# Three banks of PSUM for transposes and two for projections in a two-layer decoder trunk

## The chip, the cores and the metric

The kernel runs on one core of a Trainium2 chip. The metric is the device time of one execution in microseconds. Five engines take part: TensorE (PE in the profile; its weight loads are PEld), VectorE (DVE), ScalarE (ACT), GpSimd (POOL) and SyncE (SP), which issues most transfers. In this kernel every result of TensorE lands in one of eight PSUM banks of 128 x 512 fp32, and VectorE or ScalarE reads it out before the bank is used again.

## The reference

Two layers over x of 512 x 1024, fp32. In each, four groups of four attention heads read one input projection, one output projection follows, and then a SwiGLU FFN; RMSNorm stands before and after both.

```python
for l in range(DEPTH):                                  # 2
    h = rmsnorm(x, g_pre_mix[l])
    z = jnp.einsum('bsd,de->bse', h, w_in[l])           # 1024 -> 2660
    o_moba = moba_attention(rope(qa), rope(ka), va)     # with 512 keys: causal over all of them
    o_fox = blocked_causal_attention(qb, kb, vb, HEAD_DIM ** -0.5, cumsum(log_sigmoid(z_fg + b)))
    o_mla = blocked_causal_attention(q_full, k_full, v_c, 96 ** -0.5)   # ranks 192 and 128, up-projected
    o_dil = dilated_mixture(rope(qd), rope(kd), vd)
    y = jnp.einsum('bse,ed->bsd', mix, w_out[l])
    x = x + rmsnorm(y, g_post_mix[l])
    h = rmsnorm(x, g_pre_ffn[l])
    f = silu(h @ w_gate[l]) * (h @ w_up[l])             # 1024 -> 2816
    x = x + rmsnorm(f @ w_down[l], g_post_ffn[l])
```

## The kernel before

Every fp32 product is made of three matmuls: both sides are split into a high part (ScalarE's cast, whi, lat_hi, sp_hi) and the rest (VectorE or GpSimd, wlo, lat_lo, sp_lo), and mm3 (L196 to L198) adds high x high, low x high and high x low. Tokens stand in four row blocks of 128. A tile scheduler sets the order of each engine's instructions from the program, the pools' sizes and its own costs; the program's text sets only what may be overlapped, and a generator mechanism (run, steps with prices) lays projections of the next head group between the steps of the attention heads.

PSUM is shared by four pools, each tile a whole bank: ps_mm (3 banks) for projections, ps_s (2) for scores, ps_t (2) for transposes, ps_o (1) for a head's output. The order of work in one layer:

- *Opening.* For each row block, hn = x scaled by rstd and gain (VectorE, L214), eight transposes into two hnT tiles (ps_t, L222), and h split from them (L230). Then for each row block the values of the fox heads (ps_v, ps_mm, 24 matmuls of 256 columns, drained by ScalarE L307 and VectorE L308) and the latents (ps_lat, 24 of 356 columns). In layer 0 the rope tables (L251 to L271) are made on VectorE meanwhile. Fox queries and keys follow (ps_qk, 24 of 512 columns, into q_stk, kh_stk, klz).
- *Up-projections of mla* (L653 to L669): per row block ps_qup (five matmuls) and ps_kvup (three), drained by ScalarE and VectorE into nat and v. The cumulated forget gates go through ps_cum, cumT, crow (L702) and GpSimd's casts into klz (L707), the second operand of the fox scores.
- *Heads*, two at a time: scores ps_s (two terms, L460), row maximum (L463), exp (L465), GpSimd's scaling pr (L475), transposes pT (L484) in turns of three or four into ps_t, split into pta and ptb (L486, L487), and ps_o (L492, L493). mla heads begin with transposes natT (L678, ps_t). The order of groups is fox, mla, moba, dilated; projections of later groups stand between, and the output projection ps_out stands among the dilated heads.
- *FFN.* Half-blocks ps_g and ps_u over the first two blocks of 128 columns (halves), then pairs of blocks in seven products each (two_blocks), then the down-projection into eight accumulators ps_d that hold all eight banks.

The places that the change touches are the pools at L90 to L92, the list halves at L835 and the list acc at L959.

Of the kernel before, what the change touches and what calls it, by code (L numbers as in the profile page):

```python
# [14 lines left out]
PSUM = bass.MemoryType.PSUM  # L15
# [66 lines left out]
def decoder(ctx, tc, x, positions, w_in, b_forget, g_mla_q, w_mla_q_up, g_mla_kv, w_mla_kv_up,  # L82
# [4 lines left out]
    keep = ctx.enter_context(tc.tile_pool(name="keep", bufs=1))  # L87
    wp = ctx.enter_context(tc.tile_pool(name="wp", bufs=1))
    small = ctx.enter_context(tc.tile_pool(name="small", bufs=8))
    ps_mm = ctx.enter_context(tc.tile_pool(name="ps_mm", bufs=3, space=PSUM))  # L90
    ps_s = ctx.enter_context(tc.tile_pool(name="ps_s", bufs=2, space=PSUM))
    ps_t = ctx.enter_context(tc.tile_pool(name="ps_t", bufs=2, space=PSUM))  # L92
    ps_o = ctx.enter_context(tc.tile_pool(name="ps_o", bufs=1, space=PSUM))

    def bank(pool, name):
        return pool.tile([P, 512], F32, name=name, tag=pool.name)
# [13 lines left out]
    def slot(tag, dt, name):  # L110
        n = 6 if tag == "E" else 4
        return keep.tile([P, n, 512], dt, name=name, tag="slot" + tag)[:, 0:4, :]
# [37 lines left out]
    def gain(src, l, queue=nc.scalar):  # L150
        g = [R(F32, "gain") for _ in range(2)]
        for c in range(2):
            queue.dma_start(g[c], src[l:l + 1, 512 * c:512 * c + 512].broadcast_to([P, 512]))
        return g
# [4 lines left out]
    def weights(src, shape, into=None):  # L159
        raw = wp.tile([P] + shape, F32, name="wraw", tag="wraw", bufs=WRAW)  # L160
        if into is None:
            hi = wp.tile([P] + shape, F32R, name="whi", tag="whi", bufs=WSPL)
            lo = wp.tile([P] + shape, F32R, name="wlo", tag="wlo", bufs=WSPL)
        else:
            hi, lo = into
        nc.sync.dma_start(raw, src)
        nc.scalar.copy(hi, raw)  # L167
        chunk_no[0] += 1
        if pool_share[0] and chunk_no[0] % pool_share[0] == 0:
            nc.gpsimd.tensor_tensor(lo, raw, f32(hi), op=ALU.subtract)  # L170
        else:
            nc.vector.tensor_tensor(lo, raw, f32(hi), op=ALU.subtract)  # L172
        return hi, lo
# [641 lines left out]
    def ffn(l, xt, h, turns, f_slots, after):  # L815
# [5 lines left out]
        def w_of(src, j, into=(None, None)):  # L821
            cs = slice(j * P, (j + 1) * P)
            return [weights(src[l, 4 * i * P:4 * (i + 1) * P, cs].rearrange("(k p) c -> p k c", p=P), [4, P], into=into[i])
                    for i in range(2)]

        def block(ps, w, hs):
            for k in range(KD):
# [5 lines left out]
        room = keep.tile([P, 6, 512], F32R, name="w_half", tag="slotE")  # L833
        room = [room[:, i, :].rearrange("p (k c) -> p k c", c=P) for i in range(4)]
        halves = [(bank(ps_mm, "ps_g"), w_of(w_gate, 0)), (bank(ps_mm, "ps_u"), w_of(w_up, 0)),  # L835
                  (bank(ps_mm, "ps_g"), w_of(w_gate, 1)), (bank(ps_o, "ps_u"), w_of(w_up, 1, (room[0:2], room[2:4])))]
        for hs in (slice(0, 256), slice(256, 512)):
            for i, (ps, w) in enumerate(halves):
                block(ps, w, hs)
# [116 lines left out]

        tail = 4
        gpost = gain(g_post_ffn, l)
        acc = [[bank(p, "ps_d") for p in ps] for ps in ((ps_t, ps_t), (ps_s, ps_s), (ps_mm, ps_mm), (ps_mm, ps_o))]  # L959

        def load(j, into=None, w_into=(None, None)):
            fh, fl = into or (T(F32R, "fh"), T(F32R, "fl"))
# [13 lines left out]
        room = [q[:, i, :] for tag in ("M2", f_slots[0], f_slots[3]) for q in [slot(tag, F32R, "tail")] for i in range(4)]  # L976
# [54 lines left out]
    for l in range(depth):  # L1031
        pool_share[0] = SHARE_MIX
        xt, h, turns = mixing(l, h, set_a, set_b, w_first if l == 0 else None)
        nxt = []

        def after(t):
            dst = out[0] if l + 1 == depth else x_mid[l]
            for c in range(2):
                nc.sync.dma_start(dst[t * P:(t + 1) * P, 512 * c:512 * c + 512], xt[t][c])
            if l + 1 < depth:  # L1040
                if not nxt:
                    nxt.append(gain(g_pre_mix, l + 1))
                    nxt.append(new_h(set_b))
                pre_norm(t, xt[t], nxt[0], nxt[1])

        ffn(l, xt, h, turns, set_a, after)
        if nxt:
            h = nxt[1]
        set_a, set_b = set_b, set_a
# [21 lines left out]
```

## Time and profile before

| | us |
|---|---|
| median of 3 runs | 1247.77 (1247.18 to 1248.88) |
| the profiled execution | 1246.28 |
| its span | 1244.3 |
| TensorE busy | 1212.3 (97%) |
| VectorE busy | 892.3 (72%) |
| ScalarE busy | 667.9 (54%) |
| GpSimd busy | 243.7 (20%) |

Busy time is that of one engine over the whole span. Matmuls are pipelined, so each is listed longer than the distance to the next start. A number in brackets in a timeline is the engine's idle time before that instruction, with the instruction that ended it. Tiles are named out<-in.

### The profile page before, as it was taken

The page shows a single profiled execution, that of the slowest core. Times are in us where ns is not written, and L with a number is a line of the kernel's source. Part 1 is how long each engine was busy: PE and PEld are TensorE (multiplying, and loading weights), DVE is VectorE, ACT ScalarE, POOL GpSimd, SP SyncE. Part 2 cuts the span into 40 slices and gives each one's busy share as a digit, 9 for nine tenths or more (in the row PEclk, how much of TensorE's full clock was granted, in tenths as well). Part 3 has the DMA queues.
Part 4 walks back from the last instruction along what each step waited for, and adds up shares of the span by engine and source line. Part 5 has one row for each costly group of instructions (what it writes and reads, how often), then busy time and mean ns, then how long its engine had stood idle before and what let it go on. Part 6 is the DMA issues. An engine that isn't in the chain of part 4 may idle for free.

```text
span 1244.3 us, 20754 instructions
## 1 busy us (share of the span) xinstructions
PE 1212.3 (97%) x7372; PEld 1069.7 (86%) x7372; DVE 892.3 (72%) x1802; ACT 667.9 (54%) x1453; POOL 243.7 (20%) x337
## 2 busy tenths in 40 slices
PE   8999999999999999999989999999899999999997
PEld 7878877779999999888788788778799999998886
DVE  6877877788988788533467778677789887893334
ACT  6676766754544445333446767576554544453332
POOL 3343443343000000000242524333430000000001
PEclk9999999999999999999999999999999999999999
DMA  7221232521433333433443222334224333333331
GB/s 230 77 61 43 74 112 70 162 68 35 136 95 101 113 101 102 136 94 94 134 118 77 52 60 77 100 94 129 69 68 125 109 99 102 103 114 116 99 94 71
DMA packets 158060, 121.68 MB, mean 98 GB/s; under 512 B 9090, under 2 KB 133122, under 8 KB 157956
## 3 DMA queue, kind: packets, MB, share of 16 engines
q1 hardware_dynamic: 151908, 111.55, 30.6%
q10 hardware_dynamic: 6048, 8.80, 2.5%
q8 instruction: 58, 0.95, 0.3%
q14 instruction: 46, 0.38, 0.1%
HBM read 111.93 MB, written 4.19 MB: 93 GB/s over the span
## 4 chain that ended last, share of the span: by engine, by line
PE 83%; DVE 6%; ACT 4%; issue 2%; POOL 2%; DMA 2%; ACTq 0%; DVEq 0%; POOLq 0%
PE ps L197 8%; PE ps L196 8%; PE ps L198 8%; PE ps_d L196 6%; PE ps_d L197 6%; PE ps_d L198 6%; PE ps_g L197 4%; PE ps_g L196 3%; PE ps_g L198 3%; PE ps_qk L196 3%; PE ps_s L460 3%; PE ps_qk L197 3%; PE ps_qk L198 3%; PE pT L484 2%; PE ps_out L198 1%
## 5 line engine op out<-in xcount | busy, mean ns | idle before, releaser
L172 DVE TENSOR_TENSOR wlo<-wraw,whi 128x512 fp32r<-128x512 f32 x209 | 158.2, 766 | 133.3 <-ACT whi L167 131.0
L167 ACT CAST whi<-wraw 128x512 fp32r<-128x512 f32 (+1 forms) x228 | 138.4, 620 | 172.1 <-PE ps_d L198 120.8
L891 ACT CAST whi<-wsum 128x512 fp32r<-128x512 f32 x120 | 74.4, 620 | 133.8 <-DVE wsum L897 49.2
L197 PE MATMUL ps<-sum,whi 128*128 128x256 f32 x480 | 135.8, 283 | 0.0
L196 PE MATMUL ps<-sum,whi 128*128 128x256 f32 x480 | 135.5, 282 | 0.0
L198 PE MATMUL ps<-sum,wlo 128*128 128x256 f32 x480 | 135.3, 282 | 0.0
L239 POOL TENSOR_SCALAR rstd<-ssp 128x1 f32<-128x1 f32 x16 | 6.4, 397 | 641.4 <-ACT jk L235 641.3
L196 PE MATMUL ps_d<-whi,fh 128*128 128x512 f32 x288 | 112.2, 390 | 0.0
L197 PE MATMUL ps_d<-wlo,fh 128*128 128x512 f32 x288 | 112.1, 389 | 0.0
L198 PE MATMUL ps_d<-whi,fl 128*128 128x512 f32 x288 | 112.0, 389 | 0.0
L198 PE MATMUL ps<-h,wlo 128*128 128x256 f32 x360 | 101.9, 283 | 0.0
L197 PE MATMUL ps<-h,whi 128*128 128x256 f32 x360 | 101.9, 283 | 0.0
L196 PE MATMUL ps<-h,whi 128*128 128x256 f32 x360 | 101.8, 283 | 0.0
L475 POOL TENSOR_SCALAR pr<-pr,den 128x128 f32<-128x128 f32 (+3 forms) x128 | 75.6, 606 | 116.8 <-DVE den L472 87.0
L198 PEld LDWEIGHTS ps<-sum,wlo 128*128 128x128 f32 x480 | 91.9, 192 | 0.0
L196 PEld LDWEIGHTS ps<-sum,whi 128*128 128x128 f32 x480 | 91.8, 191 | 0.0
L197 PEld LDWEIGHTS ps<-sum,whi 128*128 128x128 f32 x480 | 91.8, 191 | 0.0
L892 DVE TENSOR_TENSOR wlo<-wsum,whi 128x512 fp32r<-128x512 f32 x120 | 81.1, 685 | 9.6 <-ACT whi L891 8.6
L197 PE MATMUL ps_g<-h,whi 128*128 128x512 f32 (+1 forms) x224 | 81.1, 362 | 5.8 <-DVE h L230 5.8
L196 PE MATMUL ps_g<-h,whi 128*128 128x512 f32 (+1 forms) x224 | 80.9, 362 | 0.6 <-ACT h L230 0.4
L198 PE MATMUL ps_g<-h,wlo 128*128 128x512 f32 (+1 forms) x224 | 80.3, 359 | 0.0
L891 ACT CAST whi<-wraw 128x512 fp32r<-128x512 f32 x90 | 55.8, 620 | 42.3 <-PE ps L197 26.2
(321 smaller groups left out, 3507.1 us busy)
## 6 DMA issues: line engine op xcount, KB each, us to landing
wraw<-in_w_gate_dram SPq DMA_DIRECT2D x88, 256.0 KB, 3.4
wraw<-in_w_up_dram SPq DMA_DIRECT2D x88, 256.0 KB, 3.0
wraw<-in_w_down_dram SPq DMA_DIRECT2D x88, 256.0 KB, 2.8
wraw<-in_w_in_dram SPq DMA_DIRECT2D x72, 256.0 KB, 3.1
wraw<-in_w_out_dram SPq DMA_DIRECT2D x32, 256.0 KB, 2.7
xt<-in_x_dram SPq DMA_DIRECT2D x16, 256.0 KB, 3.4
rope_b<-rope_a ACTq DMA_DIRECT2D x64, 64.0 KB, 2.0
wraw<-in_w_in_dram SPq DMA_DIRECT2D x16, 178.0 KB, 3.0
```

What stands on the lines that cost most here:

```text
L167: nc.scalar.copy(hi, raw)
L172: nc.vector.tensor_tensor(lo, raw, f32(hi), op=ALU.subtract)
L196: nc.tensor.matmul(ps, a_hi, b_hi, start=start, stop=False)
L197: nc.tensor.matmul(ps, a_hi, b_lo, start=False, stop=False)
L198: last_mm[0] = nc.tensor.matmul(ps, a_lo, b_hi, start=False, stop=stop)
L239: nc.gpsimd.tensor_scalar(r, ss[:, 0:1], ss[:, 1:2], EPS, op0=ALU.add, op1=ALU.add)
L460: nc.tensor.matmul(ps[:, 0:w], a[:, qt * P:(qt + 1) * P], b[:, 0:w], start=i == 0, stop=i == n - 1)
L475: nc.gpsimd.tensor_scalar(p, p, den[:, t - qa:t - qa + 1], 1.0, op0=ALU.mult, op1=ALU.mult)
L484: nc.tensor.transpose(pt[:, i * P:(i + 1) * P], pr[:, offs[qt] + kt * P:offs[qt] + (kt + 1) * P], ident)
L891: nc.scalar.copy(hi, raw)
L892: nc.vector.tensor_tensor(lo, raw, f32(hi), op=ALU.subtract)
```

## The change

One bank goes from the pool of projections to the pool of transposes. Two tiles that were the third user of ps_mm get other pools: the FFN's third half-block takes a bank of ps_s, and one accumulator of the down-projection the third bank of ps_t. No instruction is added or taken away.

```diff
-    ps_mm = ctx.enter_context(tc.tile_pool(name="ps_mm", bufs=3, space=PSUM))
+    ps_mm = ctx.enter_context(tc.tile_pool(name="ps_mm", bufs=2, space=PSUM))
     ps_s = ctx.enter_context(tc.tile_pool(name="ps_s", bufs=2, space=PSUM))
-    ps_t = ctx.enter_context(tc.tile_pool(name="ps_t", bufs=2, space=PSUM))
+    ps_t = ctx.enter_context(tc.tile_pool(name="ps_t", bufs=3, space=PSUM))
...
-                  (bank(ps_mm, "ps_g"), w_of(w_gate, 1)), (bank(ps_o, "ps_u"), w_of(w_up, 1, (room[0:2], room[2:4])))]
+                  (bank(ps_s, "ps_g"), w_of(w_gate, 1)), (bank(ps_o, "ps_u"), w_of(w_up, 1, (room[0:2], room[2:4])))]
...
-        acc = [[bank(p, "ps_d") for p in ps] for ps in ((ps_t, ps_t), (ps_s, ps_s), (ps_mm, ps_mm), (ps_mm, ps_o))]
+        acc = [[bank(p, "ps_d") for p in ps] for ps in ((ps_t, ps_t), (ps_s, ps_s), (ps_mm, ps_mm), (ps_t, ps_o))]
```

The scheduler sets another order from it. The excerpts give instructions as line, operation, out<-in and shape.

First excerpt: TensorE in the opening of layer 0, between the second and third row block's transposes; the lines with - are gone from here, those with + have come.

```order
-L196 MATMUL ps_v<-whi,h 128x256
 L196 MATMUL ps_lat<-lat_hi,h 128x356
-L222 MATMUL hnT<-cst,hn 128x128 x4
-L197 MATMUL ps_v<-wlo,h 128x256
-L222 MATMUL hnT<-cst,hn 128x128 x4
+L222 MATMUL hnT<-cst,hn 128x128 x8
 L197 MATMUL ps_lat<-lat_lo,h 128x356
 L198 MATMUL ps_lat<-lat_hi,h 128x356
```
The ps_v matmuls of the second row block that stood here stand after the fourth row block's transposes now.

Second excerpt: VectorE in the same opening, at the drain L308 of the third row block's values (ps_v_427), among the rope table's passes (pos, posi, angn, kn). Before:

```order
L255 TENSOR_SCALAR angn_631<-cst_79,posn_623 128x16 x4
L261 TENSOR_SCALAR posi_624<-pos_622 128x512
L308 TENSOR_TENSOR v_262<-ps_v_427,v_262 128x2x128
L261 TENSOR_SCALAR kn_636<-angn_631 128x64
L262 TENSOR_SCALAR posi_624<-posi_624 128x512
L262 TENSOR_SCALAR kn_636<-kn_636 128x64
```
After:

```order
L264 SCALAR_TENSOR_TENSOR pos_622<-posi_624,pos_622 128x512
L268 TENSOR_SCALAR kn_636<-kn_636 128x64
L264 SCALAR_TENSOR_TENSOR pos_622<-posi_624,pos_622 128x512
L308 TENSOR_TENSOR v_262<-ps_v_427,v_262 128x2x128
L264 SCALAR_TENSOR_TENSOR pos_622<-posi_624,pos_622 128x512
L265 TENSOR_SCALAR pos_622<-pos_622 128x512
L266 TENSOR_SCALAR posi_624<-pos_622 128x512
```
The drain stood behind the first step on pos and stands behind three of its four subtractions L264 now.

Third excerpt: TensorE in the up-projections of layer 0; ps_s_901 and ps_s_906 are the first two score tiles of the fox heads, klz00 their second operand. Before, from the end of the first ps_kvup:

```order
L198 MATMUL ps_kvup_779<-whi_748,sp_lo_682 128x512
L691 MATMUL ps_cum_861<-fg_602,cst_79 128x16
L691 MATMUL ps_cum_861<-fg_602,ones_85 128x12
L691 MATMUL ps_cum_861<-fg_602,ones_85 128x8
L691 MATMUL ps_cum_861<-fg_602,ones_85 128x4
L460 MATMUL ps_s_901<-kh_stk_725,q_stk_590 128x256
L196 MATMUL ps_qup_787<-whi_734,sp_hi_677 128x384
L197 MATMUL ps_qup_787<-wlo_735,sp_hi_677 128x384
L198 MATMUL ps_qup_787<-whi_734,sp_lo_678 128x384
```
After, from the end of the first ps_qup:

```order
L691 MATMUL ps_cum_861<-fg_602,ones_85 128x4
L460 MATMUL ps_s_901<-kh_stk_725,q_stk_590 128x256
L460 MATMUL ps_s_906<-kh_stk_725,q_stk_590 128x256
L196 MATMUL ps_kvup_779<-whi_748,sp_hi_681 128x512
L197 MATMUL ps_kvup_779<-wlo_749,sp_hi_681 128x512
L198 MATMUL ps_kvup_779<-whi_748,sp_lo_682 128x512
L700 MATMUL cumT_871<-cst_79,cpad_107 128x128
L678 MATMUL natT_879<-cst_79,nat_753 96x128
L678 MATMUL natT_888<-cst_79,nat_753 96x128
L460 MATMUL ps_s_901<-klz00_99,fox_q_552 128x256
L460 MATMUL ps_s_906<-klz00_99,fox_q_552 128x256
```
Both terms of the first scores, the transpose cumT and two transposes natT have moved ahead of the second ps_qup, and the first ps_kvup behind the scores' first terms.

Fourth excerpt: TensorE where the moba heads end and the dilated heads begin; ps_o_2427 is the output of a dilated pair, pta what its transposes become, ps_qk projections. Before:

```order
L198 MATMUL ps_qk_2389<-h_124,wlo_2385 128x512
L492 MATMUL ps_o_2427<-pta_859,v_860 128x512
L484 MATMUL pT_2488<-cst_79,pr_2225 128x128 x3
L493 MATMUL ps_o_2427<-pta_859,v_860 128x512
L196 MATMUL ps_qk_2481<-h_123,whi_2470 128x512
L197 MATMUL ps_qk_2481<-h_125,whi_2470 128x512
```
After:

```order
L197 MATMUL ps_qk_2481<-h_125,whi_2470 128x512
L198 MATMUL ps_qk_2481<-h_123,wlo_2471 128x512
L484 MATMUL pT_2488<-cst_79,pr_2225 128x128 x3
L196 MATMUL ps_qk_2481<-h_123,whi_2470 128x512
L492 MATMUL ps_o_2427<-pta_859,v_860 128x512
L197 MATMUL ps_qk_2481<-h_125,whi_2470 128x512
L198 MATMUL ps_qk_2481<-h_123,wlo_2471 128x512
L493 MATMUL ps_o_2427<-pta_859,v_860 128x512
```
Six projections ps_qk_2481 more stand ahead of the first ps_o_2427 now (three of them are shown), and pT_2488 stands ahead of it too.

## Rows read from the trace of the kernel before

**Rows 1.** the page: busy time of each engine, granted clock in 40 slices, chain by engine
```profile
PE 1212.3 (97%) x7372; PEld 1069.7 (86%) x7372; DVE 892.3 (72%) x1802; ACT 667.9 (54%) x1453; POOL 243.7 (20%) x337
PEclk9999999999999999999999999999999999999999
PE 83%; DVE 6%; ACT 4%; issue 2%; POOL 2%; DMA 2%; ACTq 0%; DVEq 0%; POOLq 0%
```

**Rows 2.** stretches: length, then busy us of PE, PEld, DVE, ACT, POOL, granted clock
```profile
320.00:340.00 20.00, 20.00 (x161) 19.66 (x160) 19.47 (x40) 9.68 (x20) 0.00 (x0) 1.00 0.49 138
...
560.00:580.00 20.00, 20.00 (x90) 16.56 (x89) 6.92 (x12) 6.66 (x12) 0.00 (x0) 1.00 0.29 92
```

**Rows 3.** what PE waited for: total us, times, longest us
```profile
PE ps_g L197 <- DVE h L230: 5.8, 4, 1.9
...
PE pT L484 <- POOL pr L475: 2.4, 9, 0.3
```

**Rows 4.** timeline of PE, opening of layer 0: start, duration, line, tiles, idle before
```profile
21.33 0.28 PE L198 MATMUL ps_v<-whi,h 128*128 128x256 f32 x1
...
22.17 0.28 PE L196 MATMUL ps_v<-whi,h 128*128 128x256 f32 x1
...
24.04 0.43 PE L197 MATMUL ps_lat<-lat_lo,h 128*128 128x356 f32 x1 [0.19 <-DVE lat_lo L172]
```

**Rows 5.** timeline of DVE, opening of layer 0
```profile
21.66 1.39 DVE L214 SCALAR_TENSOR_TENSOR hn<-xt,rstd,gain 128x512 f32<-128x512 f32 x2
...
37.08 0.42 DVE L308 TENSOR_TENSOR v<-ps_v,v 128x256 fp32r<-128x256 f32 x1
...
45.47 0.41 DVE L308 TENSOR_TENSOR v<-ps_v,v 128x256 fp32r<-128x256 f32 x1
```

**Rows 6.** timeline of PE, the stretch before the first up-projection
```profile
38.84 0.33 PE L196 MATMUL ps_lat<-lat_hi,h 128*128 128x356 f32 x1
...
42.74 0.39 PE L196 MATMUL ps_qk<-h,whi 128*128 128x512 f32 x1
...
56.01 0.44 PE L198 MATMUL ps_qup<-whi,sp_lo 128*128 128x384 f32 x1 [0.23 <-DVE sp_lo L623]
57.32 0.44 PE L655 MATMUL ps_qup<-whi,q_stk 128*128 128x384 f32 x1 [0.88 <-DVE q_stk L629]
```

**Rows 7.** timelines of PE and then DVE, opening of layer 1
```profile
640.67 0.63 PE L222 MATMUL hnT<-cst,hn 128*128 128x128 f32 x4 [0.91 <-DVE hn L214]
...
641.11 0.41 DVE L308 TENSOR_TENSOR v<-ps_v,v 128x256 fp32r<-128x256 f32 x1
```

**Rows 8.** timelines of DVE, POOL and PE, first two fox heads
```profile
65.38 0.68 DVE L702 TENSOR_TENSOR crow<-cumT,cst 128x512 fp32r<-128x512 f32 x1
...
66.20 2.75 POOL L707 CAST klz<-crow 64x512 fp32r<-64x512 f32 x4 [8.19 <-DVE t L644]
...
72.66 0.79 PE L484 MATMUL pT<-cst,pr 128*128 128x128 f32 x2 [0.24 <-POOL pr L475]
73.68 0.55 PE L484 MATMUL pT<-cst,pr 128*128 128x128 f32 x3 [0.23 <-POOL pr L475]
```

**Rows 9.** timeline of PE: an mla head, the change-over, its like in layer 1
```profile
109.57 0.64 PE L678 MATMUL natT<-cst,nat 128*96 128x128 f32 x4 [0.88 <-DVE ptb L487]
...
178.72 0.38 PE L493 MATMUL ps_o<-ptb,v 128*128 128x256 f32 x1 [0.66 <-DVE ptb L487]
...
186.49 0.66 PE L484 MATMUL pT<-cst,pr 128*128 128x128 f32 x4 [0.34 <-POOL pr L475]
...
195.76 0.47 PE L492 MATMUL ps_o<-pta,v 128*128 128x512 f32 x1 [0.48 <-ACT pta L486]
...
811.41 0.47 PE L492 MATMUL ps_o<-pta,v 128*128 128x512 f32 x1 [0.48 <-ACT pta L486]
```

**Rows 10.** stretches after the long waits at the opening of layer 1
```profile
632.00:634.00 2.00, 2.00 (x11) 2.00 (x11) 1.97 (x4) 1.02 (x3) 0.77 (x2) 0.50 0.25 75
634.00:636.00 2.00, 2.00 (x15) 2.00 (x15) 1.43 (x3) 2.00 (x5) 0.68 (x1) 0.88 0.07 11
```

## The prediction

> **What bounds the kernel now.** I read the page's busy times and slices first [rows 1]. TensorE is busy 1212.3 of 1244.3 us, so only about 32 us of its span are idle, and the time can change by what happens to those 32 us and to little else. Next come the stretches. In the middle of the FFN and of the down-projection TensorE is busy 20.00 of 20.00 us [rows 2]; there is nothing to win there, and a bank can cost something there only if TensorE runs out of it. The waits then say where the idle time lies [rows 3]: matmuls ps_g at the FFN's start wait for the normalised h, transposes pT wait for probabilities that GpSimd scales. Neither of these two releasers is a bank. So I walked TensorE's new order through every place where the old one stood still, with the trace's times for VectorE, ScalarE and GpSimd.
>
> One reading rule is needed. A 256-wide ps_v matmul lasts 0.28 us, but from 21.33 to 22.17 seven of them start 0.12 us apart [rows 4]. A bracketed idle is counted from the end of the matmul before, so a hole costs about 0.28 - 0.12 = 0.16 us more than its bracket says. I add that to each.
>
> **The change part by part.** No instruction is added or removed. The two moved banks (third half-block of the FFN, one of eight accumulators of the down-projection) name other banks at places where the old order shows no wait for a bank; the work before them is the end of attention, or the FFN, and their groups run for microseconds. I cost them at 0. If that cover is gone, one drain of a bank, 0.41 us [rows 5], is the price, so 0 to +0.8 in two layers. What is left is the order.
>
> *Opening of layer 0.* In the old order ps_v matmuls of the second row block stand between projections ps_lat and transposes hnT, in the third projection bank. With two banks they can't begin before the first ps_v is drained, and the order puts all 24 after the fifth last ps_lat group. Of them 21 filled waits: for hn, which VectorE makes from 21.66 to 23.05 [rows 5], and for lat_lo, the hole at 24.04 [rows 4]. TensorE now waits for these times idle and runs the 21 later: 21 x 0.12 = **+2.5 us**. This is the firmest term. Further on, ps_v of the fourth block needs the bank of the third, whose VectorE drain L308 now stands behind three passes of the rope table (see the second excerpt). It ran at 37.08 before [rows 5]; three passes of about 0.7 us put it near 39.3. TensorE comes at 38.5: the 24 ps_v end at 38.84, where ps_lat takes over [rows 6], so they began 24 x 0.12 earlier, at 36.0, and all is 2.5 late. That is up to +0.9, and 0 if the rope work ends earlier. The next bank, for ps_qk, needs the drain that ran at 45.47 [rows 5] and now has two weight splits in front: 0 to +0.7. I take +1.4 of the 1.6, since VectorE has no idle stretch there. Against this stand old waits that a late TensorE no longer sees: at 56.01 (0.23 + 0.16) and 57.32, where 1.31 us pass for a 384-wide matmul. A 356-wide one takes (42.74 - 38.84) / 24 = 0.16, so this needs about 0.18, and the hole is 1.13 [rows 6]. They wait for ScalarE and VectorE on q_stk and sp_lo, whose queue is full and doesn't start later. That gives back 1.5. Net **+2.4**, with ends +1.0 (no further bank wait) and +4.1 (nothing given back).
>
> *Opening of layer 1.* The same filling, but seven ps_v only, ahead of the wait for hn at 640.67; the first ps_v bank is drained by VectorE at 641.11 [rows 7], after that wait. 7 x 0.12 = **+0.8**.
>
> *Up-projections and first two fox heads.* The old order ran four pairs of ps_qup and ps_kvup densely over three banks. The new one sets score matmuls between them (third excerpt). The second term of the first score needs klz: cumT, then crow on VectorE (0.68 us), then GpSimd's cast, 2.75 us for four, so 0.69 each [rows 8]. From the transpose to the score that is about 1.4 to 1.6 us, and little is left to fill it: +1.2 to +1.5. Two-bank drains add some 0.3 to 0.6. In return the waits of pT for pr at 72.66 and 73.68 (0.24 and 0.23, each + 0.16 [rows 8]) and one like them ahead go, since the softmax starts earlier: about -1.2. I take **+0.7**, and **+0.5** in layer 1; ends 0 and +1.2 each.
>
> *Further transposes in attention.* Two waits per layer of pT for pr, of the nine in the list of waits [rows 3], have a third bank's worth of slack in the new order: **-0.4** each, -0.8. The wait of natT for the drain of ptb at 109.57 (0.88 + 0.16 [rows 9]) shrinks by a group of transposes, 0.4, but fewer projections are left behind it: **-0.2** in all.
>
> *The moba to dilated change-over.* Here the third transpose bank pays. At 178.72 ps_o waits for ptb (0.66 + 0.16): its last transposes now stand twelve or more projections earlier, so this goes. At 186.49 pT waits for pr (0.34 + 0.16): other transposes and two projections come first, so this mostly goes. At 195.76 ps_o waits for pta (0.48 + 0.16): six more 512-wide ps_qk, over 1.3 us, come between its transposes and it (fourth excerpt), so this goes [rows 9]. That is 1.96 us; I take -1.8. Layer 1 has the same at 811.41 [rows 9] and a like one for pr, but hardly any at the first place: -1.4. Together **-3.2**, ends -4.0 and -1.5, since each could leave a smaller wait behind it.
>
> [...] The output projection's small waits are only shuffled: 0, with ends -1 and +1.
>
> Sum: +2.4 + 0.8 + 1.2 - 0.8 - 0.2 - 3.2 - 0.3 = **-0.1 us**. The profiled run took 1246.28 us (span 1244.3 and 2.0 around it), so 1246.2 by it; the median of the three runs is 1247.77, so I predict **1247.7 us**.
>
> **The rivals.** *Slower: banks starve the projections.* The lateness of the opening isn't given back, because the fox q chain (ps_qk, ScalarE, VectorE, q_stk) moves along with TensorE: then the 1.5 us at 56 to 57 stay, and the up-projections cost 1.2 in both layers. Sum: -0.1 + 1.7 + 1.2 = +2.8, about 1250.6, and up to 1252 with the change-over at its lower gain. For it: VectorE holds the drains in a full queue. Against it: ScalarE has other work ahead of these casts. It decides at the hole at 57.32: if after it has a hole there too, this rival holds.
>
> *Slower: the clock falls.* After the long waits around 630 the granted clock was 0.50 from 632 to 634 and 0.88 from 634 to 636 [rows 10]: 2 x 0.50 + 2 x 0.12 = 1.2 us lost. In the new opening TensorE stands idle for about the same sum, 2.5 us around 21 to 24, in three pieces, and at 640 for 0.8 longer. Falls at both places give +2.4, so 1250.1 and with any loss beside it over 1250.3. Against it: the waits at the FFN's start, up to 1.9 us long [rows 3], left no fall in the page's slices. [...]
>
> *Faster: only the transposes count.* The opening keeps only 1.0 and the up-projections nothing, while the change-over gives 4.0 and natT another 0.8: +1.0 + 0.8 - 0.8 - 1.0 - 4.0 - 0.3 = -4.3, about 1243.5. For it: every wait of the change-over [rows 9] hangs on a transpose that a third bank lets in earlier. Against it: the 21 + 7 fillers of the openings have no other cover.
>
> *Nothing: the change doesn't do what it says.* TensorE would be fed by something else in all these places, and reordering would shift idle time without changing its sum: 1247.8, within 0.3. Against it: at 640.67 and at 21 to 24 the order alone takes cover away.
>
> **How the numbers follow.** Offsetting terms as summed: 0.42, its own range 1245.4 to 1250.2. Nothing: 0.08. Starved banks: 0.20. Clock: 0.07. Faster: 0.23. A measurement of this kernel can tell 0.2%, or 2.5 us, from no change, so same is 0.42 + 0.08 = 0.50, slower 0.20 + 0.07 = 0.27, faster 0.23. The range reaches from the faster rival's time to that of the starved banks at its worst: 1243.5 to 1252.0.
>
> **What would show it.** In the changed trace: no ps_v between 17 and 24 us, holes of about 2.5 us in all there and one some 0.8 longer ahead of hnT near 640; a wait of ps_s for klz after the first ps_kvup; ps_qup with q_stk no longer waiting near 57; no wait of ps_o for ptb near 179 and for pta near 196; busy 20.00 of 20.00 in the FFN as before. A wait for a bank inside the FFN or the down-projection, or a granted clock below 1.00 at 24 us, would make the sum wrong; so would holes that stay at 186 and 196, since the whole balance rests on them.

## The result and the profile after

The changed kernel takes 1256.53 us (median of six runs, 1254.12 to 1259.12) against 1248.33 us for the kernel before (six runs, 1247.18 to 1251.42): a ratio of 1.0067, 95% interval 1.0054 to 1.0080. It is slower, by about 8 us. The prediction was 1247.7 us with a range up to 1252.0; the measured time lies 4.5 us above that.

The page of the changed kernel, in the lines that answer to [rows 1]; its profiled span is 9.1 us longer:

```profile
span 1253.4 us, 20758 instructions
PE 1211.3 (97%) x7372; PEld 1070.9 (85%) x7372; DVE 895.5 (71%) x1802; ACT 667.7 (53%) x1453; POOL 244.1 (19%) x337
PE 81%; DVE 7%; ACT 3%; POOL 3%; DMA 3%; issue 2%; SPq 0%; ACTq 0%; DVEq 0%; POOLq 0%
```

TensorE is busy as long as before, 1211.3 us for 1212.3. So the 9 us are idle time, and the question is where. (Each of the two traces has one fall of the granted clock ahead of its last 3 us: to 0.50 from 632 to 634 us before [rows 10], to 0.52 from 280 to 282 us in the changed kernel.) For that I compare the two traces at equal work: the times at which TensorE has done the same amount of matmul work, each matmul counted with the usual distance between two starts of its shape. The difference of the two times is how late the changed kernel is, and its growth over a stage is what that stage lost. Times of stages are those of the kernel before. Where the two orders differ, a figure depends on where the cut falls, by up to 0.2 us.

| stage (us of before) | predicted | changed kernel | again (experiment 9) |
|---|---|---|---|
| opening of layer 0 (to 58) | +2.4 | +3.49 | +1.97 |
| up-projections, first two fox heads (to 79) | +0.7 | +0.99 | +2.32 |
| other fox heads, mla (to 172) | -0.6 | -0.66 | -0.66 |
| moba to dilated (to 201) | -1.8 | +0.11 | -0.79 |
| output projection (to 250) | 0 | +0.76 | +0.71 |
| FFN's start (to 288) | 0 | +1.87 | +2.35 |
| FFN, down-projection (to 608) | 0 | +0.09 | +0.10 |
| opening of layer 1 (to 652) | +0.8 | +0.45 | +0.57 |
| up-projections, fox (to 736) | +0.1 | +0.19 | +1.48 |
| mla, moba to dilated (to 821) | -1.4 | -0.91 | -0.78 |
| output projection (to 856) | 0 | +2.22 | +2.21 |
| FFN's start (to 912) | 0 | +0.46 | +1.89 |
| the rest | 0 | +0.03 | +0.05 |

(The last term of the prediction's sum, -0.3 for fewer changes between transposes and matmuls, had no place of its own.) The last column is the ninth experiment below, the same kernel profiled once more. The opening's holes, in the timeline of TensorE in the changed kernel:

```profile
17.87 0.43 PE L196 MATMUL ps_lat<-lat_hi,h 128*128 128x356 f32 x1 [1.22 <-ACT lat_hi L167]
...
22.44 1.28 PE L222 MATMUL hnT<-cst,hn 128*128 128x128 f32 x8 [1.04 <-DVE hn L214]
23.98 0.43 PE L197 MATMUL ps_lat<-lat_lo,h 128*128 128x356 f32 x1 [0.26 <-DVE lat_lo L172]
...
39.31 0.39 PE L196 MATMUL ps_v<-whi,h 128*128 128x256 f32 x1 [0.72 <-DVE v L308]
...
47.88 0.50 PE L196 MATMUL ps_qk<-h,whi 128*128 128x512 f32 x1 [1.52 <-DVE v L308]
```

The waits for hn and lat_lo answer to [rows 4]: without ps_v beside them they stand open, as predicted. So does the first and largest, for the high part that ScalarE makes (lat_hi), which the prediction did not name: ten of its 21 fillers had stood in front of it. The last two are waits for a bank, whose drains L308 have moved, as VectorE's timeline shows, from 37.08 and 45.47 [rows 5] to

```profile
38.84 0.42 DVE L308 TENSOR_TENSOR v<-ps_v,v 128x256 fp32r<-128x256 f32 x1
...
44.62 1.53 DVE L575 SCALAR_TENSOR_TENSOR lat<-lat,r,gqkv 128x192 f32<-128x192 f32 x1 [2.31 <-POOL r L574]
...
46.34 1.15 DVE L172 TENSOR_TENSOR wlo<-wraw,whi 128x512 fp32r<-128x512 f32 x2
47.41 0.41 DVE L308 TENSOR_TENSOR v<-ps_v,v 128x256 fp32r<-128x256 f32 x1
```

At 47.41 the drain stands behind two weight splits, and these behind the operation at 44.62, which waits 2.31 us for GpSimd. Near 57, where TensorE waited for q_stk [rows 6], it waits no longer: the five ps_qup matmuls start 0.18 apart from 60.26. That gave back the 1.9 us between the lateness of 5.25 at 53 and about 3.4 at 58.

At the change-over the wait for pta [rows 9, at 195.76] is gone. The one for pr, 0.34 before, has grown, and the one for ptb is nearly as it was (in this profile; it is absent from the second one of the same kernel, experiment 9):

```profile
181.10 0.39 PE L493 MATMUL ps_o<-ptb,v 128*128 128x256 f32 x1 [0.59 <-DVE ptb L487]
...
191.34 0.76 PE L484 MATMUL pT<-cst,pr 128*128 128x128 f32 x5 [0.91 <-POOL pr L475]
```

GpSimd's timeline in the changed kernel says why. It makes three of the four pr, then the low part of a mix (L540), then the fourth with the next four:

```profile
187.97 1.39 POOL L475 TENSOR_SCALAR pr<-pr,den 128x128 f32<-128x128 f32 x3 [6.25 <-DVE den L472]
189.32 1.29 POOL L540 TENSOR_TENSOR mix<-mixf,mix 128x512 fp32r<-128x512 f32 x1
190.58 2.74 POOL L475 TENSOR_SCALAR pr<-pr,den 128x512 f32<-128x512 f32 x5
```

The kernel before made all four first:

```profile
184.37 2.07 POOL L475 TENSOR_SCALAR pr<-pr,den 128x128 f32<-128x128 f32 x4 [7.32 <-DVE den L472]
186.40 1.29 POOL L540 TENSOR_TENSOR mix<-mixf,mix 128x512 fp32r<-128x512 f32 x1
```

In layer 1's output projection two holes of TensorE are new:

```profile
837.32 0.50 PE L196 MATMUL ps_out<-wearly,mix 128*128 128x512 f32 x1 [0.45 <-ACT park L752]
...
840.10 0.39 PE L492 MATMUL ps_o<-ptb,v 128*128 128x256 f32 x1 [1.58 <-DVE mixf L532]
```

The first is a wait for a drained projection bank. At the second the only output bank waits for VectorE's mixf, which is late. Before, 27 ps_out matmuls stood between this ps_o and the one ahead of it; now 20 do, and the last four of them come after the first hole. VectorE's order has changed here too. Before, mixf stood right behind a rope product:

```profile
830.21 1.08 DVE L330 TENSOR_TENSOR rope_a<-rope_a,cosT 128x512 f32<-128x512 f32 x1 [0.62 <-DMA rope_b<-rope_a]
831.32 0.42 DVE L532 TENSOR_TENSOR mixf<-ps_o,mixt 64x256 f32<-64x256 f32 x1
```

In the changed kernel a weight split and the rope sum, 2.3 us together, stand between the two:

```profile
835.63 1.78 DVE L330 TENSOR_TENSOR rope_a<-rope_a,cosT 128x512 f32<-128x512 f32 x1
837.34 1.78 DVE L172 TENSOR_TENSOR wlate<-wraw,wlate 128x512 fp32r<-128x512 f32 x1
839.04 0.68 DVE L332 TENSOR_TENSOR rope_a<-rope_a,rope_b 128x512 f32<-128x512 f32 x1
839.64 0.41 DVE L532 TENSOR_TENSOR mixf<-ps_o,mixt 64x256 f32<-64x256 f32 x1
```

So this hole has two parts that no experiment took apart: fewer fillers on TensorE, and a later mixf.

And at the FFN's start of layer 0 the granted clock has fallen, to 0.63 from 278 to 280 us and to 0.52 from 280 to 282. The stretches, columns as in [rows 2]:

```profile
278.00:280.00 2.00, 1.90 (x10) 1.83 (x10) 1.35 (x3) 0.72 (x2) 0.65 (x2) 0.63 0.03 8
280.00:282.00 2.00, 2.00 (x11) 2.00 (x11) 1.75 (x4) 0.72 (x2) 0.30 (x1) 0.52 0.00 0
...
284.00:286.00 2.00, 2.00 (x20) 2.00 (x19) 0.59 (x1) 1.39 (x4) 0.41 (x2) 1.00 0.00 0
```

Eleven matmuls run in two microseconds there, twenty at a granted clock of 1.00 from 284 to 286; those of ps_g with 256 columns start 0.21 us apart from 280.00 and 0.12 from 282.05. By the granted clock 2 x 0.37 + 2 x 0.48 = 1.7 us are lost, nearly all of that stage. In the opening of layer 1, where the kernel before lost 1.2 us in that way [rows 10], the changed kernel's profile shows a granted clock of 1.00.

### The profile page after: what moved, and what is told of

Same layout as the page of the kernel before. It is cut to its first block, busy times and chain, and to the rows that moved or that the text cites. A ratio compares the mean times of both kernels' runs of the same rounds, so it can differ in the third digit from the quotient of the medians.

```text
span 1253.4 us, 20758 instructions
## 1 busy us (share of the span) xinstructions
PE 1211.3 (97%) x7372; PEld 1070.9 (85%) x7372; DVE 895.5 (71%) x1802; ACT 667.7 (53%) x1453; POOL 244.1 (19%) x337
## 4 chain that ended last, share of the span: by engine, by line
PE 81%; DVE 7%; ACT 3%; POOL 3%; DMA 3%; issue 2%; SPq 0%; ACTq 0%; DVEq 0%; POOLq 0%
PE ps L196 8%; PE ps L197 8%; PE ps L198 8%; PE ps_d L198 6%; PE ps_d L196 6%; PE ps_d L197 6%; PE ps_g L196 4%; PE ps_g L197 3%; PE ps_g L198 3%; PE ps_qk L197 3%; PE ps_qk L196 3%; PE ps_qk L198 3%; PE ps_s L460 3%; PE pT L484 2%; POOL pr L475 2%
## 5 line engine op out<-in xcount | busy, mean ns | idle before, releaser
L172 DVE TENSOR_TENSOR wlo<-wraw,whi 128x512 fp32r<-128x512 f32 x209 | 155.2, 752 | 137.7 <-ACT whi L167 135.7
```

## The experiments

Two theories. Theory 1: the loss comes from two banks for projections, because a projection that has no bank can't fill a wait. Theory 2: it comes from the third transpose bank, because the order that it brings is worse on GpSimd and VectorE. Each kernel ran beside the kernel before, which took 1246.34 to 1246.69 us there. The changed kernel was run once more beside the last ones, 1256.43 us; where others are set against it, that is the figure.

| kernel | us | ratio to before, 95% interval |
|---|---|---|
| 1: two and two | 1260.25 | 1.0113 (1.0091 to 1.0136) |
| 2: half-block edit alone | 1246.48 | 1.0000 (0.9989 to 1.0011) |
| 3: opening's ps_v on loan | 1252.33 | 1.0051 (1.0033 to 1.0068) |
| 4: ps_out on loan | 1253.42 | 1.0057 (1.0037 to 1.0077) |
| 5: 3 and 4 together | 1250.93 | 1.0033 (1.0021 to 1.0044) |
| 6: three, and three shared | 1241.84 | 0.9961 (0.9945 to 0.9976) |
| 7: 5, and ps_kvup on loan | 1245.25 | 0.9987 (0.9976 to 0.9998) |
| 8: L540 on VectorE | 1252.14 | 1.0052 (1.0035 to 1.0069) |
| 9: the changed kernel again | 1256.43 | 1.0078 (1.0061 to 1.0094) |
| 10: 6 with 8 | 1242.37 | 0.9972 (0.9960 to 0.9984) |
| 11: 10 with ps_kvup on loan | 1240.13 | 0.9948 (0.9933 to 0.9963) |

**1. Take the third transpose bank away again.**

```diff
-    ps_t = ctx.enter_context(tc.tile_pool(name="ps_t", bufs=3, space=PSUM))
+    ps_t = ctx.enter_context(tc.tile_pool(name="ps_t", bufs=2, space=PSUM))
+    ps_x = ctx.enter_context(tc.tile_pool(name="ps_x", bufs=1, space=PSUM))
-        acc = [[...] for ps in (..., (ps_mm, ps_mm), (ps_t, ps_o))]
+        acc = [[...] for ps in (..., (ps_mm, ps_mm), (ps_x, ps_o))]
```

> The changed kernel with the third transpose bank taken away again: two banks for projections, two for transposes, and the eighth bank used only by one accumulator of the down-projection. Theory 1 (two projection banks cost, because projections that filled waits can't start): opening and output projection stay as long as in the changed kernel, and the few waits that the third transpose bank took away come back; 1256 to 1259 us. Theory 2 (the third transpose bank costs, because the new order on GpSimd and VectorE in attention is worse): only the opening's loss of 4 us or so stays; 1251 to 1253 us.

Measured 1260.25 us, above both expectations and some 4 us more than the changed kernel: theory 2 can't be the whole. Per stage it loses in the output projection of layer 1 as the changed kernel does (+2.04), and lacks its small gains: -0.07 in place of -0.83 over the other fox heads and mla to 125 us, -0.14 in place of -0.83 in the change-over of layer 1. So the third transpose bank is worth about 4 us, and the lost projection bank costs some 13. This is the clean comparison for the lost bank, since the transposes and outputs have the banks of before. It also splits the late mixf of layer 1: here mixf stands behind the rope product as before, the hole at that ps_o is 0.54 instead of 1.58, and the stage loses its 2 us at other holes (0.59 for a projection bank, 0.57 for ptb).

**2. The half-block edit alone, in the kernel before.**

```diff
-                  (bank(ps_mm, "ps_g"), w_of(w_gate, 1)), ...
+                  (bank(ps_s, "ps_g"), w_of(w_gate, 1)), ...
```

> The kernel before with one of the edits alone: the FFN's third half-block in a score bank, pools as before. Both theories: within 0.2% of before, 1246 to 1250 us. If the edit itself makes the FFN start late, 2 us more at the FFN's start, 1250 to 1251 us.

1246.48 us, ratio 1.0000. The edit is free as a whole. Its profile loses 0.4 us at the FFN's start of layer 0, by a new wait of 0.34 for ScalarE's h, and the granted clock there is 1.00; so at most that much of the 1.87 is its doing.

**3. Lend the opening a bank.** In the changed kernel:

```diff
-                ps = bank(ps_mm, "ps_v")
+                ps = bank(ps_s if c0 == C_FOX + 512 and t % 2 else ps_mm, "ps_v")
```

> The changed kernel, but the values of the second and fourth row block in the opening take a score bank, which is free there, so the opening has the banks that it had before. Theory 1: the holes of 0.9 and 1.7 us near 39 and 48 us go and some of the 2.5 us near 20; 2.5 to 4 us less than the changed kernel, 1252 to 1254 us. Rival: the holes in the opening only take the place of the wait for q_stk near 57 us, so at most 1 us less, 1255 to 1257 us.

1252.33 us, 4 us less than the changed kernel. The bank waits of 39 and 48 us are gone, and at 58 us the kernel is level with before (-0.12 us, where the changed one is 3.49 late). Theory 1 holds for the opening; the rival that these holes only take the place of the q_stk wait is out.

**4. Lend the output projection a bank.** In the changed kernel:

```diff
+            out_turn[0] += 1
-            ps = bank(ps_mm, "ps_out")
+            ps = bank(ps_t if out_turn[0] % 3 == 0 else ps_mm, "ps_out")
```

> The changed kernel, but every third tile of the output projection takes a transpose bank. Theory 1: ps_out no longer waits for a drained bank near 219, 272, 837 and 891 us, and more of it can fill the wait of ps_o near 840 us; 2 to 3.5 us less than the changed kernel, 1253 to 1255 us. Theory 2: the loss near these places comes from the order of GpSimd and VectorE; within 1 us of the changed kernel, or slower since transposes lose the bank.

1253.42 us, 3 us less, as expected in sum, but not in its places. In layer 0 the output projection gains 0.44 where the changed kernel lost 0.76. In layer 1 it loses the same 2.20: the loan fell to other tiles, and both holes stand as they were, in the timeline of TensorE:

```profile
834.82 0.50 PE L196 MATMUL ps_out<-wearly,mix 128*128 128x512 f32 x1 [0.44 <-ACT park L754]
...
837.59 0.39 PE L492 MATMUL ps_o<-ptb,v 128*128 128x256 f32 x1 [1.57 <-DVE mixf L532]
```

Another part of the 3 us is the FFN's start of layer 0, +0.55 in place of +1.87, where this profile shows a granted clock of 1.00. So what this trace shows of the loan itself is the 1.2 us in layer 0.

**5. Both loans.**

> The changed kernel with both loans of the third and fourth experiment: odd row blocks of the opening's values in a score bank, every third tile of the output projection in a transpose bank. Theory 1 (lost fillers): the two gains, 4.2 and 3.1 us, add, since the places are apart: 1249 to 1250 us beside 1246.7 of before. If both only made the same later wait shorter, no better than the better of the two, 1252 us.

1250.93 us: they add, less 1 to 2 us. The clock differs from run to run: the three of its ten runs with a granted clock of 0.998 over the span took 1248.7 to 1249.4, about the whole sum, and the profiled one, 0.991 and the slowest, 1254.5. In that one the clock fell five times (near 62, 274, 636, 680 and 895 us), to 0.50 to 0.56 in the lowest stretch of 2 us of each.

**6. Three for projections, three shared by transposes and outputs.** In the kernel before:

```diff
-    ps_t = ctx.enter_context(tc.tile_pool(name="ps_t", bufs=2, space=PSUM))
-    ps_o = ctx.enter_context(tc.tile_pool(name="ps_o", bufs=1, space=PSUM))
+    ps_t = ctx.enter_context(tc.tile_pool(name="ps_t", bufs=3, space=PSUM))
+    ps_o = ps_t
```

> Three banks for projections as before, and the transposes and the heads' output share three (two and one before); scores keep two. Theory 1: the projections keep their fillers, so none of the losses; the transposes may use a third bank when no output holds it: 1243 to 1247 us. Theory 2 (more banks for transposes make the order of GpSimd and VectorE worse): 1248 to 1252 us.

1241.84 us, below the expectation's lower end and faster than both kernels. The change-over alone gives -1.80 in layer 0 and -1.82 in layer 1, about what was predicted of the third transpose bank, though here the outputs too may take a second bank. Here GpSimd makes all four pr in one piece, the mix ahead of them, and TensorE has one hole from 172 to 202 us. GpSimd and then TensorE:

```profile
180.10 1.30 POOL L540 TENSOR_TENSOR mix<-mixf,mix 128x512 fp32r<-128x512 f32 x1 [2.86 <-ACT mix L539]
182.83 2.07 POOL L475 TENSOR_SCALAR pr<-pr,den 128x128 f32<-128x128 f32 x4 [1.43 <-DVE den L472]
...
179.29 0.50 PE L460 MATMUL ps_s<-klz,q_stk 128*128 128x256 f32 x2 [0.40 <-DVE klz L357]
```

The output projection of layer 1 loses nothing (-0.06). Nor do the two other kernels with these pools (10: -0.06, 11: -0.05), while the eight profiles of kernels with two projection banks lose 2.0 to 2.3 there. VectorE's mixf is as late in these three as in the changed kernel (behind the same split and rope sum), and TensorE has no hole. But two things differ: a third projection bank, and outputs that are no longer bound to one bank, so that ps_o need not wait for mixf. No kernel has the second without the first. That the projection bank alone suffices for a loss of 2 us there is shown by experiment 1; which of the missing fillers would have to come back was not isolated.

**7. Lend the up-projections a bank too.** To experiment 5:

```diff
-            ps = bank(ps_mm, "ps_kvup")
+            ps = bank(ps_t, "ps_kvup")
```

> As the fifth experiment, and ps_kvup in transpose banks too, so that up-projections have a third bank again and stand densely. Theory 1: the waits for klz and the fall of the clock that sometimes follows them near 66 and 682 us go: 1.5 to 3 us less than the fifth experiment, 1246 to 1248 us. Rival: ps_kvup only takes the bank from the transposes natT and cumT, which wait in its place; no change against the fifth, 1249 to 1250 us.

1245.25 us, more than expected: 5.7 us less than experiment 5, and a little faster than before although projections have two banks of their own. The stage to 79 us goes from +2.52 to -0.10, that to 736 us from +2.84 to -1.15. Part of both is the clock, which fell at 62 and 680 us in experiment 5 and is 1.00 in every stretch of this profile up to 1236 us. Over all ten runs of each, the mean granted clock is 0.9982 here and 0.9955 there, up to 3.4 of the 5.7 us. The wait for klz, in the timeline of TensorE in the changed kernel:

```profile
65.72 0.50 PE L460 MATMUL ps_s<-klz,fox_q 128*128 128x256 f32 x2 [0.57 <-POOL klz L707]
```

and in this experiment:

```profile
69.51 0.51 PE L460 MATMUL ps_s<-klz,fox_q 128*128 128x256 f32 x2 [0.28 <-POOL klz L707]
```

**8. Take the mix out of the fourth pr's way.** In the changed kernel:

```diff
-                nc.gpsimd.tensor_tensor(ml[:, cols], mf[:, 0:ncol], f32(mh[:, cols]), op=ALU.subtract)
+                (nc.vector if e == 0 else nc.gpsimd).tensor_tensor(ml[:, cols], ...)
```

> The changed kernel, but the low part of the first moba pair's mix (L540, 1.29 us on GpSimd, two layers) is made on VectorE, so that it no longer stands ahead of the fourth pr. If GpSimd's order caused the 0.9 us waits of pT near 191 and 810 us, these fall below 0.4 and the kernel is 0.8 to 1.5 us faster than the changed one, 1255 to 1255.8 us. If the probabilities were late for another reason (exp on ScalarE, the reciprocal), the waits stay.

1252.14 us, 4 us less where at most 1.5 was expected. The cause is confirmed: GpSimd makes four pr in one piece, and TensorE's wait at the place is 0.35 instead of 0.91:

```profile
186.45 2.48 POOL L475 TENSOR_SCALAR pr<-pr,den 128x128 f32<-128x128 f32 x4 [6.25 <-DVE den L472]
...
188.32 0.55 PE L484 MATMUL pT<-cst,pr 128*128 128x128 f32 x3 [0.35 <-POOL pr L475]
```

The change-over now gives -1.45 and -1.63. Against the first profile of the changed kernel that is 1.6 and 0.8 us, but 0.9 of the 1.6 is the wait for ptb, which the ninth experiment lacks without this edit. Against that one the edit returned 0.7 and 0.8 us, the 1.5 that was expected at most. The rest of the 4 us isn't this edit: 1.3 us is the FFN's start of layer 0, where the granted clock is 1.00 from 278 to 282 us in this profile, 0.6 that of layer 1, and 0.6 the opening, whose later holes differ from run to run.

**9. The changed kernel again.**

> The changed kernel once more, unchanged, beside the last variants, to see which of its losses repeat. By theory 1 the losses of the opening (5.2 us at the 50th us), of the output projection and of the up-projections repeat to 0.1 us; what a fallen clock costs (1.7 us near 280 us in the first profile) may stand at another place or not at all. 1254 to 1258 us.

1256.43 us: the time repeats. The loss of the 21 fillers (2.46 us in the first profile, 2.34 here) and the output projection repeat to about 0.1 us (last column of the first table). The opening as a whole doesn't: the bank wait at 39 is gone, that for ps_qk is 1.14 where it was 1.52, since VectorE's rope work came earlier by itself, with L308 at 37.33 and 45.91 us. At the change-over the wait for ptb is gone, as the prediction had it (so it is in experiments 3, 4 and 5), and the stage gives -0.79 in place of +0.11. The one for pr stands as it was:

```profile
190.30 0.76 PE L484 MATMUL pT<-cst,pr 128*128 128x128 f32 x5 [0.90 <-POOL pr L475]
```

And the clock fell at four places in place of one, among them the up-projections of both layers; the stretches:

```profile
64.00:66.00 2.00, 1.80 (x6) 1.80 (x7) 1.21 (x6) 1.69 (x5) 1.88 (x4) 0.50 0.00 0
...
280.00:282.00 2.00, 2.00 (x11) 2.00 (x11) 1.45 (x3) 0.72 (x2) 0.84 (x2) 0.50 0.00 0
686.00:688.00 2.00, 2.00 (x8) 2.00 (x8) 0.65 (x4) 1.25 (x6) 1.18 (x3) 0.50 0.00 0
900.00:902.00 2.00, 2.00 (x12) 2.00 (x11) 1.91 (x4) 0.60 (x2) 0.00 (x0) 0.51 0.00 0
```

**10 and 11. The sixth with the edits of the eighth, then of the seventh too.**

> The sixth experiment (three banks for projections, three shared by transposes and outputs) with the first moba pair's L540 on VectorE as in the eighth. In the sixth the order on GpSimd at the change-over is that of before, four pr ahead of L540, so little is left to win there: theory 1: within 1 us of the sixth, 1241 to 1243 us, 1 us less only if the wait of pT for pr near 186 us goes.

> The tenth experiment with ps_kvup in the shared transpose banks as in the seventh. Theory 1: with three projection banks the up-projections already stand densely, so the loan brings no more than 1 us: 1240 to 1243 us. If in the seventh the gain came from the order of the scores behind the up-projections and not from the bank, it is found here too: 1237 to 1240 us.

1242.37 us: no more than the sixth, as expected, since GpSimd's order was good there. With ps_kvup in the shared banks 1240.13 us, the fastest of all, 0.5% below the kernel before:

```profile
span 1237.8 us, 20746 instructions
PE 1205.7 (97%) x7372; PEld 1071.1 (87%) x7372; DVE 894.5 (72%) x1804; ACT 666.8 (54%) x1453; POOL 239.6 (19%) x335
```

It lies at the border of the two expectations. The stage to 79 us gives -0.74 and that to 736 us -1.52, with a granted clock of 1.00 in both, against +0.05 and -0.21 in the tenth. So the loan is worth about 2 us even where projections have three banks: it is more than a repair.

## Why the prediction was wrong

*What bounds the kernel* was right: no time moved in the middle of the FFN or the down-projection (+0.09 in 320 us), and the balance was decided at places where TensorE waits.

*The opening of layer 0*, +2.4 predicted, +3.49 in the profiled run. The mechanism held piece by piece: 2.5 us for the 21 fillers (measured 2.46), up to 0.9 for the first bank wait (0.88), the old q_stk holes given back (1.5 predicted, 1.9 found). The term mis-sized was the second bank wait, 0.7 predicted and 1.7 measured: the two splits ahead of the drain stood behind an operation that itself waited 2.31 us for GpSimd. In the ninth experiment this wait was shorter by 0.4 us and the first one absent, so the term has a spread of over 1 us that one trace doesn't show.

*The opening of layer 1*, +0.8 predicted: the wait at 640.67 [rows 7] is 1.66 instead of 0.91, at 646.84 in the changed kernel, so the size was right. The stage shows +0.45, because before's own trace had lost 1.2 us to the clock close by [rows 10] and after's had not, and another wait for lat_lo (0.36) came.

*The up-projections*, +0.7 and +0.5 predicted: +0.99 in layer 0 and, with the fox heads' gain, +0.19 where +0.1 was summed in layer 1. Right in the profiled run. In the ninth experiment the clock fell in these waits and they cost 1.3 us more each.

*The change-over*, -3.2 predicted, about -0.8 found in the first profile and -1.6 in the second, is **the step that failed first**. The prediction followed TensorE's order to where the transposes come earlier and took the waits for gone. It didn't look at the order of the engines that TensorE waits for there. GpSimd's had changed too, and put 1.29 us of L540 ahead of the fourth pr: the wait at 186 that was to go mostly (0.34) grew to 0.91, in both layers and both profiles. The wait for pta went as predicted. The one for ptb went in the second profile and stayed in the first, where VectorE's drain of it, behind a rope operation, ended a microsecond later; that 0.9 us is a spread between runs. Experiment 8 shows that L540 was the miss: with the four pr in one piece the two layers give -3.1, which is the size predicted.

*The output projection*, "only shuffled: 0", +0.76 and +2.22 found, is **the second**. It was called even without a walk through its order, though it is where two banks hold unfinished projections that wait for late heads. In layer 1, 27 ps_out matmuls covered the wait for the output bank before and 20 do now; TensorE waits 0.45 for a drain and then 1.58 for VectorE, whose own order has also become worse there. Experiment 1 ties the loss of the stage to the lost projection bank (+2.04 without the third transpose bank); how the 1.58 divides between fewer fillers and the later mixf is not shown.

*The FFN's start*, 0 predicted, +1.87 and +0.46 found. The bank waits there are 0.3 to 0.8 us. The rest was the clock. In the twelve profiles other than that of the kernel before the stage to 288 us cost +1.5 to +2.4 in the seven where the clock fell, and +0.2 to +0.6 in the five where it didn't; the stage to 912 us +1.6 to +2.0 in the five with a fall, -0.4 to +0.5 in the seven without. The rival "the clock falls" named the price well (1.2 us, about 1.4 here), but the wrong places: not the opening of layer 0, but the FFN's start and, in five of the eight profiles of kernels with two projection banks, the up-projections. It was given 0.07; the row that it was dismissed by, a full clock at the FFN's start of before, is one profile's, and other profiles have a fall there. Nor could the page's slices have shown one: the slice that holds before's own fall at 632 is a 9 like the others [rows 1]. That the lost bank brings the falls at the FFN's start is not shown: two of the five profiles with three projection banks have one there in layer 0, as have five of the eight with two. Nor are the falls most of the loss: over ten runs of the changed kernel the mean granted clock is 0.9951, over 49 of the kernel before 0.9976, which is 3.1 us of the 10 at most; and runs of equal clock, 0.998, took 1255.2 and 1255.5 us with the change and 1245.0 to 1247.4 without. In the seven profiles of two-bank kernels with interleaved up-projections the clock fell seven times in these, to 0.50 to 0.56 in the lowest stretch of each; in the six profiles with dense ones it is 1.00 there. Through the rest of attention it is 1.00 in all thirteen, and the largest terms are plain waits.

*The last term of the sum*, -0.3 for changes between transposes and matmuls, is shown by no run. The trace of the kernel before shows 0.01 us in the median for a change and back, over 78 groups of transposes with no idle time around them, beyond the usual distances between starts (0.109 us for a transpose, 0.120, 0.175 and 0.227 for a matmul of 256, 384 and 512 columns). The changed kernel has seven such pairs fewer, under 0.1 us together.

*The rivals.* "Starved banks" was the right side and mechanism, but for the wrong reason: its point of decision, a hole left near 57 us, went against it, and its loss came in the output projection instead. The chance of slower, 0.27, was too low because every gain of the sum rested on one trace of TensorE's order, while the losses rested on the missing bank itself. Against the prediction's sum of -0.1 the first trace has +9.1: change-over 2.4 (0.9 of it the wait for ptb that did not repeat), output projection 3.0, FFN's start 2.3, opening 1.1, the rest 0.4.

What stays open: why the clock falls in one run of a kernel and not in the next after the same wait, and whether the hole at 840 us would close with more fillers, an earlier mixf or a second output bank.

## What to carry to other kernels

A pool's last bank is worth what the scheduler fills with it: count the work that stands in the third bank while TensorE would wait, and expect that wait back, up to its whole length (for the 21 fillers of the opening 2.46 us). When a change re-orders the program, a wait on TensorE is gone only if the engine that ends it has kept or improved its own order (the wait for pr was 0.91 us with L540 ahead of the fourth pr, 0.35 without), so read the rows of the releasing engine, not of the waiting one. And before a bank is moved from one pool to another, see whether two pools whose peaks differ in time can share it: three shared by transposes and outputs, with projections keeping theirs, gave 0.4% and, with ps_kvup in them too and L540 on VectorE, 0.5%.

## What the runs showed of the hardware

The clock's falls were less settled than one trace said: by the granted clock each took 1.2 to 1.7 us (one, near 680 us in experiment 5, 3.4), and the same kernel had one of them in one profile and four in another. All came in or after idle time of TensorE, of different kinds: one wait of 2.6 us in the opening of layer 1, one of 1.9 us with shorter ones ahead of it at the FFN's start, pieces of 0.2 to 0.6 us in the up-projections; and after each of these kinds other profiles have no fall. One of VectorE's weight splits took 1.78 us beside one of GpSimd's that took 1.74; in the changed kernel, on VectorE and GpSimd:

```profile
837.34 1.78 DVE L172 TENSOR_TENSOR wlate<-wraw,wlate 128x512 fp32r<-128x512 f32 x1
...
836.83 1.74 POOL L170 TENSOR_TENSOR wlate<-wraw,wlate 128x512 fp32r<-128x512 f32 x1
```

The 169 splits of this shape (L172) in the trace that no GpSimd instruction overlaps took 0.67 to 0.69 us each, the 59 that one overlaps 0.66 to 1.78, 22 of them over 1.00. The 1.1 us by which the one at 837.34 is longer than those alone are part of the 1.58 us for which TensorE waits at 840.10.
